# Second attention: GpSimd stores the outputs and makes the mLSTM's norm

## The chip, the cores and the metric

The kernel runs on one core of a Trainium2 chip. The metric is the device time of one execution in microseconds; for the kernel before it is 3558.35 us, the median of three runs (3557.78 to 3562.14).

## What is computed

Two transformer blocks on 2048 tokens of width 1024, all in float32. The first block (a Fourier branch beside grouped attention) and the end of the second (a mixture of experts and a gated embedding) are not touched. The part of the second block that matters here has two branches, whose outputs stand side by side and go through one output projection `w_o`:

```
def second_block(x, ...):
        attn_out = _mla_attention(q_nope, q_rope, k_nope, k_rope, v)   # 8 heads, mask in chunks of 64
        xc = jax.nn.silu(_causal_conv(x_m, conv_w[i], conv_b[i]))
        mq, mk, mv = (per head: xc @ w_mq, xc @ w_mk * 128**-0.5, x_m @ w_mv)      # 4 heads of 128
        hm = _mlstm_chunkwise(mq, mk, mv, ig, fg).transpose(0, 2, 1, 3)
        mu = jnp.mean(hm, axis=-1, keepdims=True)
        var = jnp.mean(jnp.square(hm - mu), axis=-1, keepdims=True)
        hm = ((hm - mu) * lax.rsqrt(var + EPS)).reshape(B, S, ML_W) * mh_norm_g[i]
        ml_out = (hm + ml_skip[i] * xc) * jax.nn.silu(z)
        x = x + jnp.concatenate([attn_out, ml_out], axis=-1) @ w_o[i]
```

## The kernel before

The program is a chain of phases; each is a Python generator, and the first steps of the next phase (its loads) are issued while the one before still runs. The change lies in `phase_g`, which computes both branches at once, and in `mlstm`, the generator that it steps beside itself.

**Attention.** A unit is one head and one block of 512 queries (32 units, `u`). A step is one tile of 128 keys of a unit (320 steps). In each step TensorE makes the scores in three matmuls (L1281 to L1283, into `ps`), ScalarE takes the exponential (L1285, `pe`) and rounds it (L1287, `ph`), VectorE makes the rest (L1294, `pl`), and four steps later TensorE multiplies with the values (L83 to L85, `acc`). Ahead of the scores TensorE and VectorE find the maximum of each query row (L1257 into `pmx`, L1258); its negative is sent by a small DMA from GpSimd's queue into a row of the query tile (L1272, `t<-nm`). When a unit is through, `ending` copies `acc` to `o` (L1316), turns the row of sums by DMA (L1319), takes reciprocals, sends them out and back as a broadcast (L1322, L1325, `rc`), multiplies on GpSimd (L1327) and stores to `MIX2` from SP's queue (L1329). The numbers that it yields say after how many steps each piece comes: nine in all.

**The mLSTM.** An item is one chunk of 128 tokens and two of the four heads (32 items, one about every nine steps). Its stages come at fixed steps after its first (`after`): `load` (four loads on SP's queue into a pool of three buffers), `decay` (L1533 on GpSimd), `project` (L1546; `qw` on GpSimd, L1552), `turn`, `weigh`, `combine` (L1587, L1588, which read `qw` and the state), `divide` (L1603), `update`, `center`, `square` (sums of squares on ScalarE, L1633), `spread` (variance on VectorE, L1639; power -0.5 on GpSimd, L1640), `shift` (L1646 on VectorE, `mv`), `norm` (L1653, two activations on ScalarE), `gate` (transposes on TensorE, L1661; skip term on GpSimd, L1665; L1666 on VectorE; product with the gate on GpSimd, L1667) and `store` (L1674, from SP's queue).

Every engine runs its own instructions in order, and so does each queue that issues DMAs. The order isn't quite that of the code: a scheduler in the framework places the instructions of each engine by its own estimates, with the code's order as the priority. When no step but the endings is left, `phase_g` closes its inner pools and starts the loads of `w_o` for the projection behind it (`e.beside(then)`).

Of the kernel before, what the change touches and what calls it, by code (L numbers as in the profile page):

```python
# [10 lines left out]
F32 = mybir.dt.float32  # L11
# [7 lines left out]
EPS = 1e-6  # L19
# [1109 lines left out]
def phase_g(e, then):  # L1129
# [20 lines left out]
    with ExitStack() as st:  # L1150
# [161 lines left out]
        def ending(u):  # L1312

            h, b = divmod(u, NB)
            o = wk.tile([65, QB], F32, name="o", bufs=3)
            nc.scalar.activation(o, A.pop(u), AF.Copy)  # L1316
            yield 1
            rr = sm.tile([16, QB // 16], F32, name="rr")
            nc.sync.dma_start(rr, o[64:65, :].rearrange("p (a b) -> p a b", a=16))  # L1319
            yield 2  # L1320
            nc.vector.reciprocal(rr, rr)
            nc.sync.dma_start(RD2[u].rearrange("(a b) -> a b", a=16), rr)  # L1322
            yield 2
            rc = wk.tile([64, QB], F32, name="rc", bufs=2)
            nc.sync.dma_start(rc, bcast_row(RD2[u], 64, QB))  # L1325
            yield 3
            nc.gpsimd.tensor_tensor(o[0:64], o[0:64], rc, op=ALU.mult)  # L1327
            yield 1
            nc.sync.dma_start(MIX2[h * 64:(h + 1) * 64, b * QB:(b + 1) * QB], o[0:64])  # L1329

# [9 lines left out]

        turns = []
        later = {}
# [25 lines left out]
        for n in range(-LEAD, len(steps) + LAG):  # L1368
# [15 lines left out]
            if beside and next(beside, True):  # L1384
                beside = None
            if not beside and not queue and not turns and not any(f is not step_ending for x in later.values() for f, a in x) and then:
                inner.close()
                e.beside(then)
                then = None
# [91 lines left out]
def mlstm(e, pool, psum, steps):  # L1481
# [12 lines left out]
    cst = pool("h_cst", 1)  # L1494
    xp = pool("h_x", 3)
    wk = pool("h_wk", 2)
# [5 lines left out]
    nc.gpsimd.memset(mask, 0.0)  # L1502
    nc.gpsimd.affine_select(out=mask, in_=mask, pattern=[[1, CL]], compare_op=ALU.is_ge, fill=-1e30, base=0, channel_multiplier=-1)
    taps = cst.tile([128, 4, 2], F32, name="taps")
    for i, n in enumerate(("mh_norm_g_2", "ml_skip_2")):
        nc.sync.dma_start(taps[:, :, i], d[n][0].rearrange("(h p) -> p h", p=128))
    state = [cst.tile([128, 130], F32, name=f"C{h}") for h in range(4)]
    for h in range(4):
        nc.gpsimd.memset(state[h], 0.0)
    wm = cst.tile([128, 3, 4, 128], F32, name="wm")  # L1510
    for i, n in enumerate(("w_mq_2", "w_mk_2", "w_mv_2")):
        nc.sync.dma_start(wm[:, i], d[n][0].rearrange("h d e -> d h e"))
    V.tensor_scalar(wm[:, 1], wm[:, 1], 128.0 ** -0.5, None, op0=ALU.mult)
    R = {}

    def load(x):
        ci, h0 = x
        t0 = ci * CL
        xm = xp.tile([128, 2, CL], F32, name="xm")
        xc = xp.tile([128, 2, CL], F32, name="xc")  # L1520
        for T, w in ((XM, xm), (XC, xc)):
            nc.sync.dma_start(w, T[h0 * 128:(h0 + 2) * 128].rearrange("(h p) s -> p h s", p=128)[:, :, t0:t0 + CL])
        negm = xp.tile([128, 2, CL], F32, name="negm")
        wint = xp.tile([128, 2, CL], F32, name="wint")
        for T, w in ((MR, negm), (WI, wint)):
# [110 lines left out]
    def spread(x):  # L1636

        xc, hm, mu, var, zs = R[x]
        V.tensor_scalar(var, var, 1.0 / CL, EPS, op0=ALU.mult, op1=ALU.add)  # L1639
        nc.gpsimd.tensor_tensor(var, var, e.mhalf[:, :2], op=ALU.pow)  # L1640
        R[x] = (xc, hm, mu, var, zs)

    def shift(x):
        xc, hm, mu, var, zs = R[x]
        mv = sm.tile([128, 2], F32, name="mv")
        V.tensor_mul(mv, mu, var)  # L1646
        R[x] = (xc, hm, mv, var, zs)

    def norm(x):
        ci, h0 = x  # L1650
        xc, hm, mv, var, zs = R[x]
        for i in range(2):
            nc.scalar.activation(hm[:, i], hm[:, i], AF.Identity, scale=var[:, i:i + 1], bias=mv[:, i:i + 1])  # L1653
        R[x] = (xc, hm, zs)

    def gate(x):
# [10 lines left out]
        nc.gpsimd.tensor_tensor(o, o, zs, op=ALU.mult)  # L1667
        R[x] = o

    def store(x):  # L1670
        ci, h0 = x
        o = R.pop(x)
        r = slice(512 + h0 * 128, 512 + (h0 + 2) * 128)
        nc.sync.dma_start(MIX2[r].rearrange("(h p) s -> p h s", p=128)[:, :, ci * CL:(ci + 1) * CL], o)  # L1674

    stages = (load, decay, project, turn, weigh, combine, divide, update, center, square, spread, shift, norm, gate, store)
    after = (0, 5, 7, 9, 11, 13, 14, 15, 15, 16, 17, 21, 22, 24, 26)
    items = [(ci, h0) for ci in range(NC) for h0 in (0, 2)]
# [811 lines left out]
```

## Time and profile before

| what | us |
|---|---|
| median of three runs | 3558.35 |
| the profiled execution, whole | 3560.11 |
| its span (first to last instruction) | 3558.4 |
| TensorE busy in the span | 3340.2 (94%) |
| VectorE, ScalarE, GpSimd busy | 2427.9, 2052.8, 688.9 |
| the stretch of `phase_g` | about 1918 to 2590 |

Busy time is a sum over the span; what limits the kernel in a stretch is read from what ended each engine's idle time there. An engine's wait is put down to the event that came last.

### The profile page before, as it was taken

Reading aid. Unit: us, or ns where it says so; the run is one execution under the profiler, and the core shown is the slowest. Engines: PE = TensorE matmul, PEld = TensorE weight load, DVE = VectorE, ACT = ScalarE, POOL = GpSimd, SP = SyncE. Lnnn points to the kernel's source line nnn. Section 1 sums busy time; section 2 is a strip of 40 time slices with the busy share of each in tenths; the row PEclk is TensorE's granted clock in tenths of the full one; section 3 lists DMA queues with packets and bytes.
Section 4 is the critical chain, followed back from the end, with each engine's and each line's share of the span. In section 5 each row is a group of like instructions: output and inputs, shape, how many; then the busy total and the mean of one; then the engine's idle time right before and its main releaser. Section 6 shows DMA issues by size and latency. Waiting matters only on the chain. (4 is left out here: it accounts for less than half of the span.)

```text
span 3558.4 us, 48779 instructions
## 1 busy us (share of the span) xinstructions
PE 3340.2 (94%) x16556; PEld 2592.6 (73%) x16557; DVE 2427.9 (68%) x4600; ACT 2052.8 (58%) x3672; POOL 688.9 (19%) x729
## 2 busy tenths in 40 slices
PE   8999999999999998999986998988999989899798
PEld 6788766666666666889975777766778767677687
DVE  5835768888888865464454887877856657877654
ACT  4442357777777783243223777877833467777533
POOL 0000000000000000000022433433200046655332
PEclk9999999999999998999997999999999989999999
DMA  5333322101111026443247533332255578878753
GB/s 160 102 122 105 95 71 72 51 22 54 34 45 44 26 63 197 146 139 112 75 127 187 106 79 77 84 69 60 83 167 167 211 263 309 342 301 302 276 195 130
DMA packets 312984, 468.82 MB, mean 132 GB/s; under 512 B 66455, under 2 KB 201384, under 8 KB 304416
## 3 DMA queue, kind: packets, MB, share of 16 engines
q1 hardware_dynamic: 293174, 404.26, 36.6%
q0 software_dynamic: 19520, 60.97, 4.7%
q8 instruction: 148, 2.42, 0.3%
q14 instruction: 142, 1.16, 0.1%
HBM read 333.81 MB, written 135.24 MB: 132 GB/s over the span
## 5 line engine op out<-in xcount | busy, mean ns | idle before, releaser
L519 DVE TENSOR_REDUCE mx<-pmx 128x1 f32<-128x512 f32 x512 | 344.5, 685 | 85.0 <-PE pmx L518 78.8
L588 DVE TENSOR_TENSOR pl<-pe,ph 128x1024 fp32r<-128x1024 f32 (+1 forms) x272 | 340.5, 1253 | 88.5 <-ACT ph L581 87.1
L579 ACT ACTIVATE pe<-ps 128x1024 f32<-128x1024 f32 (+1 forms) x272 | 278.7, 1025 | 147.2 <-PE ps L577 137.1
L581 ACT ACTIVATE ph<-pe 128x1024 fp32r<-128x1024 f32 (+1 forms) x272 | 287.4, 1058 | 7.4
L576 PE MATMUL ps<-t,kh 128*128 128x512 f32 (+1 forms) x544 | 239.6, 440 | 0.8 <-ACT pe L579 0.8
L1294 DVE TENSOR_TENSOR pl<-pe,ph 128x512 fp32r<-128x512 f32 (+1 forms) x320 | 211.6, 664 | 39.5 <-ACT ph L1287 36.9
L74 DVE TENSOR_TENSOR gl<-raw,gh 128x512 fp32r<-128x512 f32 x256 | 222.1, 915 | 19.0 <-ACT gh L73 18.6
L577 PE MATMUL ps<-t,kl 65*128 65x512 f32 (+1 forms) x544 | 222.9, 410 | 0.0
L602 PE MATMUL acc<-ph,vh 128*65 128x512 f32 (+1 forms) x544 | 217.5, 400 | 0.0
L604 PE MATMUL acc<-pl,vh 128*65 128x512 f32 (+1 forms) x544 | 215.1, 396 | 0.0
L603 PE MATMUL acc<-ph,vl 128*65 128x512 f32 (+1 forms) x544 | 215.0, 395 | 0.0
L518 PE MATMUL pmx<-kh,t 128*128 128x512 f32 x512 | 207.4, 410 | 1.7 <-DVE mx L519 1.1
L1258 DVE TENSOR_REDUCE mx<-pmx 128x1 f32<-128x512 f32 (+2 forms) x320 | 190.7, 598 | 9.1 <-PE pmx L1257 8.8
L1285 ACT ACTIVATE pe<-ps 128x512 f32<-128x512 f32 (+1 forms) x320 | 167.0, 523 | 30.7 <-PE ps L1283 27.5
L1287 ACT ACTIVATE ph<-pe 128x512 fp32r<-128x512 f32 (+1 forms) x320 | 179.5, 564 | 6.5
L74 POOL TENSOR_TENSOR dl<-sd,dh 128x512 fp32r<-128x512 f32 x128 | 165.4, 1313 | 80.4 <-ACT dh L73 77.8
L1281 PE MATMUL ps<-t,kh 113*128 113x512 f32 (+1 forms) x320 | 136.0, 425 | 35.7 <-ACT pe L1285 28.9
L83 PE MATMUL pm<-uhi,fh 128*128 128x256 f32 x512 | 146.0, 286 | 7.4 <-ACT ev L956 3.9
L73 ACT ACTIVATE gh<-raw 128x512 fp32r<-128x512 f32 x256 | 141.1, 621 | 13.0 <-PE p L85 9.4
L84 PE MATMUL pm<-ulo,fh 128*128 128x256 f32 x512 | 144.6, 283 | 0.0
L85 PE MATMUL pm<-uhi,fl 128*128 128x256 f32 x512 | 144.2, 284 | 0.3 <-DVE fl L77 0.3
L626 POOL TENSOR_TENSOR rc<-rc,ag 128x512 f32<-128x512 f32 x16 | 23.9, 1495 | 608.0 <-DMA rc<-scr_RD 561.6
(545 smaller groups left out, 9641.7 us busy)
## 6 DMA issues: line engine op xcount, KB each, us to landing
raw<-in_w_gate_e SPq DMA_DIRECT2D x32, 1024.0 KB
raw<-in_w_up_e SPq DMA_DIRECT2D x32, 1024.0 KB
sd<-in_w_down_e SPq DMA_DIRECT2D x32, 1024.0 KB
ws<-in_w_in SPq DMA_DIRECT2D x80, 256.0 KB
xt<-in_x SPq DMA_DIRECT2D x32, 512.0 KB
scr_X<-y SPq DMA_DIRECT2D x32, 512.0 KB
xt<-scr_X SPq DMA_DIRECT2D x32, 512.0 KB
yy<-scr_Y POOLq DMA_DIRECT2D x32, 512.0 KB, 4.7
```

Source lines behind the costliest of these rows:

```text
L74: (eng or nc.vector).tensor_tensor(lo, src, f32(hi), op=ALU.subtract)
L518: nc.tensor.matmul(p, t1[:, i * 128:(i + 1) * 128], kh[:, j * 512:(j + 1) * 512], start=True, stop=True)
L519: nc.vector.reduce_max(mx[:, i, j:j + 1], p, axis=AX.X)
L576: nc.tensor.matmul(p[:n, c], kh[:, k0:k0 + n], t1[:, c], start=True, stop=False)
L577: nc.tensor.matmul(p[:n, c], kl[:, k0:k0 + n], t2[:, c], start=False, stop=True)
L579: nc.scalar.activation(pe[:n], p[:n], AF.Exp, scale=0.125)
L581: nc.scalar.activation(ph[:n], pe[:n], AF.Copy)
L588: nc.vector.tensor_tensor(pl[:n], pe[:n], f32(ph[:n]), op=ALU.subtract)
L602: nc.tensor.matmul(A[u][j], vh[:n, i, :65], ph[:n, c], start=i == 0, stop=False)
L603: nc.tensor.matmul(A[u][j], vl[:n, i, :65], ph[:n, c], start=False, stop=False)
L604: nc.tensor.matmul(A[u][j], vh[:n, i, :65], pl[:n, c], start=False, stop=i == 16)
L1294: nc.vector.tensor_tensor(pl[:, c0:], pe[:, c0:], f32(ph[:, c0:]), op=ALU.subtract)
```

## The change

Four things are changed together.

1. `norm` moves from ScalarE to GpSimd, and `shift` falls away: `spread` now makes the scaled variance, the power and the two normalisations (add the negative mean, multiply by the root) as four GpSimd instructions in a row. `gate` comes at step 23 instead of 24.
2. The stores to `MIX2`, 32 of the attention and 32 of the mLSTM, are issued from GpSimd's queue right behind the product that makes their data, not from SP's some steps later.
3. The mLSTM's loads get four buffers instead of three. The three weight loads `wm` go to GpSimd's queue, the two small `taps` loads come behind the second item's loads, and the state is cleared by VectorE.
4. A unit's end is spread over fourteen steps instead of nine, with four `o` buffers; and the projection's start also waits until the last head's first unit has been stored (`NU - NB in done`).

```diff
         def ending(u):
...
-            o = wk.tile([65, QB], F32, name="o", bufs=3)
+            o = wk.tile([65, QB], F32, name="o", bufs=4)
             nc.scalar.activation(o, A.pop(u), AF.Copy)
-            yield 1
+            yield 2
             rr = sm.tile([16, QB // 16], F32, name="rr")
             nc.sync.dma_start(rr, o[64:65, :].rearrange("p (a b) -> p a b", a=16))
-            yield 2
+            yield 4
             nc.vector.reciprocal(rr, rr)
             nc.sync.dma_start(RD2[u].rearrange("(a b) -> a b", a=16), rr)
-            yield 2
+            yield 3
             rc = wk.tile([64, QB], F32, name="rc", bufs=2)
             nc.sync.dma_start(rc, bcast_row(RD2[u], 64, QB))
-            yield 3
+            yield 5
             nc.gpsimd.tensor_tensor(o[0:64], o[0:64], rc, op=ALU.mult)
-            yield 1
-            nc.sync.dma_start(MIX2[h * 64:(h + 1) * 64, b * QB:(b + 1) * QB], o[0:64])
+            nc.gpsimd.dma_start(MIX2[h * 64:(h + 1) * 64, b * QB:(b + 1) * QB], o[0:64])
+            done.append(u)
...
-            if not beside and not queue and not turns and not any(f is not step_ending for x in later.values() for f, a in x) and then:
+            if not beside and not queue and not turns and NU - NB in done and not any(f is not step_ending for x in later.values() for f, a in x) and then:
...
-    xp = pool("h_x", 3)
+    xp = pool("h_x", 4)
...
+        nc.gpsimd.dma_start(wm[:, i], d[n][0].rearrange("h d e -> d h e"))
...
-        nc.gpsimd.memset(state[h], 0.0)
-    wm = cst.tile([128, 3, 4, 128], F32, name="wm")
-    for i, n in enumerate(("w_mq_2", "w_mk_2", "w_mv_2")):
-        nc.sync.dma_start(wm[:, i], d[n][0].rearrange("h d e -> d h e"))
-    V.tensor_scalar(wm[:, 1], wm[:, 1], 128.0 ** -0.5, None, op0=ALU.mult)
+        V.memset(state[h], 0.0)
...
     def spread(x):
 
         xc, hm, mu, var, zs = R[x]
-        V.tensor_scalar(var, var, 1.0 / CL, EPS, op0=ALU.mult, op1=ALU.add)
-        nc.gpsimd.tensor_tensor(var, var, e.mhalf[:, :2], op=ALU.pow)
-        R[x] = (xc, hm, mu, var, zs)
-
-    def shift(x):
-        xc, hm, mu, var, zs = R[x]
-        mv = sm.tile([128, 2], F32, name="mv")
-        V.tensor_mul(mv, mu, var)
-        R[x] = (xc, hm, mv, var, zs)
-
-    def norm(x):
-        ci, h0 = x
-        xc, hm, mv, var, zs = R[x]
+        G = nc.gpsimd
+        G.tensor_scalar(var, var, 1.0 / CL, EPS, op0=ALU.mult, op1=ALU.add)
+        G.tensor_tensor(var, var, e.mhalf[:, :2], op=ALU.pow)
         for i in range(2):
-            nc.scalar.activation(hm[:, i], hm[:, i], AF.Identity, scale=var[:, i:i + 1], bias=mv[:, i:i + 1])
+            G.tensor_scalar(hm[:, i], hm[:, i], mu[:, i:i + 1], var[:, i:i + 1], op0=ALU.add, op1=ALU.mult)
         R[x] = (xc, hm, zs)
...
-    def store(x):
-        ci, h0 = x
-        o = R.pop(x)
         r = slice(512 + h0 * 128, 512 + (h0 + 2) * 128)
-        nc.sync.dma_start(MIX2[r].rearrange("(h p) s -> p h s", p=128)[:, :, ci * CL:(ci + 1) * CL], o)
...
+        nc.gpsimd.dma_start(MIX2[r].rearrange("(h p) s -> p h s", p=128)[:, :, ci * CL:(ci + 1) * CL], o)
...
-    after = (0, 5, 7, 9, 11, 13, 14, 15, 15, 16, 17, 21, 22, 24, 26)
+    after = (0, 5, 7, 9, 11, 13, 14, 15, 15, 16, 17, 23)
...
-            plan.setdefault(k * (steps - 28) // len(items) + a, []).append((f, x))
+            plan.setdefault(k * (steps - 25) // len(items) + a, []).append((f, x))
```

Three places show what the scheduler makes of it. In the names the digits tell tiles apart. First ScalarE in the middle of the phase, before, from an item's squares to its norm:

```order
L1633 ACTIVATE sq_20465,var_20466<-hm_20401,mu_20402 128x128
L1218 ACTIVATE t12_16806<-qf_20396 96x512
L1285 ACTIVATE pe_20452<-ps_20448 128x512
L1287 ACTIVATE ph_20454<-pe_20452 128x512
L1548 ACTIVATE qs_20474<-pmx_20469 128x256
L1550 ACTIVATE ks_20476<-pmx_20469 128x256
L1653 ACTIVATE hm_20401<-hm_20401,mv_20596,var_20466 128x128
L1285 ACTIVATE pe_20484<-ps_20480 128x512
L1653 ACTIVATE hm_20401<-hm_20401,mv_20596,var_20466 128x128
L1287 ACTIVATE ph_20486<-pe_20484 128x512
```

The norm stands five instructions behind the squares that it depends on. The same place with the change:

```order
L1634 ACTIVATE sq_20203,var_20204<-hm_20140,mu_20141 128x128 x2
L1549 ACTIVATE qs_20212<-pmx_20207 128x256
L1551 ACTIVATE ks_20214<-pmx_20207 128x256
L1285 ACTIVATE pe_20222<-ps_20218 128x512
L1287 ACTIVATE ph_20224<-pe_20222 128x512
L1285 ACTIVATE pe_20248<-ps_20244 128x512
L1287 ACTIVATE ph_20250<-pe_20248 128x512
```

Between the squares and the next scores nothing is left that comes from GpSimd. Second, GpSimd before, one item's worth:

```order
L1667 TENSOR_TENSOR o_20434<-o_20434,zs_20179 128x256
L1565 MEMSET v1_20768 128x2x2
L1640 TENSOR_TENSOR var_20466<-var_20466,mhalf_63 128x2
L1552 TENSOR_TENSOR qw_20478<-qs_20474,wint_20281 128x256
L1665 TENSOR_SCALAR o_21166<-xc_20526,taps_17346 128x128 x2
L1327 TENSOR_TENSOR o_20547<-o_20547,rc_20672 64x512
L1272 DMA t11_16805<-nm_20645 1x4x128
L1533 TENSOR_TENSOR negm_21556<-negm_21556,mask_17341 128x256
```

The power stands right behind the product of the gate and a small memset. With the change (two units end here, one shown):

```order
L1658 TENSOR_TENSOR o_19868<-o_19868,zs_19665 128x256
L1660 DMA scr_MIX2<-o_19868 128x2x128
L1534 TENSOR_TENSOR negm_21026<-negm_21026,mask_17341 128x256
L1656 TENSOR_SCALAR o_20641<-xc_20016,taps_17351 128x128 x2
L1641 TENSOR_SCALAR var_19926<-var_19926 128x2
L1642 TENSOR_TENSOR var_19926<-var_19926,mhalf_63 128x2
L1644 TENSOR_SCALAR hm_19875<-hm_19875,mu_19876,var_19926 128x128 x2
L1553 TENSOR_TENSOR qw_19962<-qs_19958,wint_19769 128x256
L1327 TENSOR_TENSOR o_19828<-o_19828,rc_20076 64x512
L1328 DMA scr_MIX2<-o_19828 64x512
```

`qw` now stands behind the whole norm, and the skip term (L1656) behind the store that frees its buffer: the three `o` buffers of the gate turn in a ring, and this one's turn is `o_19868`'s. Third, SP's queue before:

```order
L1325 DMA rc_20345<-scr_RD2 64x512
L1329 DMA scr_MIX2<-o_20195 64x512
L1526 DMA negm_21289<-scr_MR 128x2x128
L1674 DMA scr_MIX2<-o_20434 128x2x128
L1625 DMA zs_20928<-scr_ZS 128x2x128
L1210 DMA qf_21156<-scr_QNT 64x512
L1522 DMA xc_21033<-scr_XC 128x2x128
```

The loads of the coming items stand behind two stores that wait for GpSimd. With the change:

```order
L1325 DMA rc_20199<-scr_RD2 64x512
L1210 DMA qf_20696<-scr_QNT 64x512
L1211 DMA qf_20696<-scr_QRT 32x512
L1524 DMA negm_21281<-scr_MR 128x2x128
L1626 DMA zs_20913<-scr_ZS 128x2x128
L1319 DMA rr_20236<-o_20162 16x1x32
L1520 DMA xc_21023<-scr_XC 128x2x128
```

The stores are gone from it.

## Rows read from the trace of the kernel before

**Rows 1.** Busy us by stretch: PE, PEld, DVE, ACT, POOL; PE clock, DMA share, GB/s.

```profile
1918.00:2000.00 82.00, 61.84 (x306) 49.22 (x307) 55.78 (x133) 45.83 (x119) 28.11 (x39) 0.83 0.69 143
2000.00:2480.00 480.00, 438.29 (x2436) 341.34 (x2436) 386.24 (x908) 365.66 (x903) 170.32 (x221) 0.98 0.32 76
2480.00:2590.00 110.00, 106.04 (x546) 79.98 (x545) 94.00 (x198) 91.56 (x203) 23.65 (x32) 0.98 0.27 79
```

**Rows 2.** TensorE's waits, 2000 to 2500: line waited for, total us, times, longest.

```profile
PE ps L1281 <- ACT pe L1285: 25.5, 19, 3.5
PE pmx L1577 <- DVE mx L1258: 7.4, 2, 6.3
```

**Rows 3.** The longest waits of all engines, 2000 to 2500.

```profile
ACT hm L1653 <- DVE mv L1646: 70.1, 27, 8.3
POOL negm L1533 <- DMA negm<-scr_MR: 66.7, 14, 10.3
POOL o L1327 <- DMA rc<-scr_RD: 63.1, 15, 9.2
DVE mv L1646 <- POOL var L1640: 56.0, 25, 8.5
```

**Rows 4.** What SP's queue waited for, 2000 to 2500.

```profile
SPq L1674 <- POOL o L1667: 82.1, 20, 8.0
SPq L1329 <- POOL o L1327: 56.1, 23, 5.4
```

**Rows 5.** Timeline, one item: start, us, engine, instruction, idle before and its releaser.

```profile
2202.75 0.38 PE L1661 MATMUL pmx<-ident,hm 128*128 128x128 f32 x2
...
2205.19 0.73 POOL L1667 TENSOR_TENSOR o<-o,zs 128x256 f32<-128x256 f32 x1 [1.38 <-DVE o L1666]
...
2210.10 0.72 POOL L1640 TENSOR_TENSOR var<-var,mhalf 128x2 f32<-128x2 f32 x1
...
2210.85 0.33 DVE L1646 TENSOR_TENSOR mv<-mu,var 128x2 f32<-128x2 f32 x1 [2.97 <-POOL var L1640]
...
2211.22 0.49 ACT L1653 ACTIVATE hm<-hm,mv,var 128x128 f32<-128x128 f32 x1 [1.98 <-DVE mv L1646]
...
2214.37 0.50 PE L1281 MATMUL ps<-t,kh 113*128 113x512 f32 x1 [1.01 <-ACT pe L1285]
```

**Rows 6.** Groups by line: count, busy us, mean ns of one, idle before it.

```profile
L1653 ACT ACTIVATE hm<-hm,mv,var 128x128 f32<-128x128 f32 x64 | 30.6, 487 | 73.4 <-DVE mv L1646 73.4
```

**Rows 7.** The same for GpSimd, from its list.

```profile
L1665 POOL TENSOR_SCALAR o<-xc,taps 128x128 f32<-128x128 f32 x64 | 50.9, 802 | 35.9 <-DMA scr_MIX<-o 17.5 <-DMA xc<-scr_XC 14.0 <-issue 2.5
L1327 POOL TENSOR_TENSOR o<-o,rc 64x512 f32<-64x512 f32 x32 | 45.3, 1414 | 119.7 <-DMA rc<-scr_RD 99.1 <-ACT pe L1285 16.9 <-PE ps L1283 3.7
L92 POOL TENSOR_TENSOR ss<-ss,mhalf 128x1 f32<-128x1 f32 (+1 forms) x48 | 30.4, 636 | 442.8 <-DVE ss L91 318.2 <-DVE ss L106 120.0 <-ACT junk L868 4.6
L1667 POOL TENSOR_TENSOR o<-o,zs 128x256 f32<-128x256 f32 x32 | 28.6, 893 | 35.0 <-DVE o L1666 19.6 <-DVE mu L1623 15.4
L1552 POOL TENSOR_TENSOR qw<-qs,wint 128x256 f32<-128x256 f32 x32 | 25.4, 794 | 5.2 <-ACT qs L1548 3.5 <-DMA wint<-scr_WI 1.6
L1640 POOL TENSOR_TENSOR var<-var,mhalf 128x2 f32<-128x2 f32 x32 | 24.9, 778 | 5.7 <-DVE var L1639 4.6 <-ACT ks L1550 0.8
L1272 POOL DMA_DIRECT2D t<-nm x32 | 19.6, 613 | 89.9 <-DVE nm L1271 49.0 <-DVE vl L1201 20.8 <-DVE pl L1294 10.9
```

**Rows 8.** GpSimd's own DMA issue of `t<-nm`: ns min/median/max, then us to landing.

```profile
L1272 POOL DMA_DIRECT2D t<-nm x32: 518/627/633, 1919.0 to 2559.0; - x32
...
DMA to landing us min/median/max: 1.6/2.8/8.8
```

**Rows 9.** A larger DMA from GpSimd's queue, later in the kernel: KB each, us to landing.

```profile
yy<-scr_Y POOLq DMA_DIRECT2D x32, 512.0 KB, 4.7
```

**Rows 10.** Timeline at the start of the phase.

```profile
1918.97 0.62 POOL L1272 DMA_DIRECT2D t<-nm  x1 [2.45 <-DVE nm L1271]
...
1924.49 0.80 PE L1281 MATMUL ps<-t,kh 113*128 113x512 f32 x1 [5.78 <-DMA t<-nm]
```

More of the change, by code (lines that the diff above doesn't have):

```diff
@@ L1339, in phase_g @@
         beside = mlstm(e, top, lambda: pmx.tile([128, 512], F32, name="pmx"), len(steps) + LEAD - REST)
-        turns = []
+        turns, done = [], []
         later = {}
@@ L1503, in mlstm @@
     nc.gpsimd.affine_select(out=mask, in_=mask, pattern=[[1, CL]], compare_op=ALU.is_ge, fill=-1e30, base=0, channel_multiplier=-1)
+    wm = cst.tile([128, 3, 4, 128], F32, name="wm")
+    for i, n in enumerate(("w_mq_2", "w_mk_2", "w_mv_2")):
+        nc.gpsimd.dma_start(wm[:, i], d[n][0].rearrange("h d e -> d h e"))
+    V.tensor_scalar(wm[:, 1], wm[:, 1], 128.0 ** -0.5, None, op0=ALU.mult)
     taps = cst.tile([128, 4, 2], F32, name="taps")
-    for i, n in enumerate(("mh_norm_g_2", "ml_skip_2")):
-        nc.sync.dma_start(taps[:, :, i], d[n][0].rearrange("(h p) -> p h", p=128))
     state = [cst.tile([128, 130], F32, name=f"C{h}") for h in range(4)]
     for h in range(4):
-        nc.gpsimd.memset(state[h], 0.0)
-    wm = cst.tile([128, 3, 4, 128], F32, name="wm")
-    for i, n in enumerate(("w_mq_2", "w_mk_2", "w_mv_2")):
-        nc.sync.dma_start(wm[:, i], d[n][0].rearrange("h d e -> d h e"))
-    V.tensor_scalar(wm[:, 1], wm[:, 1], 128.0 ** -0.5, None, op0=ALU.mult)
+        V.memset(state[h], 0.0)
     R = {}
@@ L1526, in load @@
             nc.sync.dma_start(w, bass.AP(tensor=T.tensor, offset=T.offset + (h0 * NC + ci) * CL, ap=[[0, 128], [NC * CL, 2], [1, CL]]))
+        if x == items[1]:
+            for i, n in enumerate(("mh_norm_g_2", "ml_skip_2")):
+                nc.sync.dma_start(taps[:, :, i], d[n][0].rearrange("(h p) -> p h", p=128))
         R[x] = (xc, xm, negm, wint)
@@ L1667, in gate @@
         nc.gpsimd.tensor_tensor(o, o, zs, op=ALU.mult)
-        R[x] = o
-    def store(x):
-        ci, h0 = x
-        o = R.pop(x)
         r = slice(512 + h0 * 128, 512 + (h0 + 2) * 128)
-        nc.sync.dma_start(MIX2[r].rearrange("(h p) s -> p h s", p=128)[:, :, ci * CL:(ci + 1) * CL], o)
-    stages = (load, decay, project, turn, weigh, combine, divide, update, center, square, spread, shift, norm, gate, store)
-    after = (0, 5, 7, 9, 11, 13, 14, 15, 15, 16, 17, 21, 22, 24, 26)
+        nc.gpsimd.dma_start(MIX2[r].rearrange("(h p) s -> p h s", p=128)[:, :, ci * CL:(ci + 1) * CL], o)
+    stages = (load, decay, project, turn, weigh, combine, divide, update, center, square, spread, gate)
+    after = (0, 5, 7, 9, 11, 13, 14, 15, 15, 16, 17, 23)
     items = [(ci, h0) for ci in range(NC) for h0 in (0, 2)]
```

## The prediction

> **What bounds the kernel now.** I read the stretch table first, since the change touches one phase only. In `phase_g` TensorE is the busiest engine: from 2000 to 2480 us it is busy 438.3 of 480 us at a mean granted clock of 0.98, ScalarE 365.7, VectorE 386.2, GpSimd 170.3; before 2000 it runs at 0.83 and is busy 61.8 of 82 us [rows 1]. So the most that any edit of the waiting can give back in the middle is TensorE's 41.7 idle us and a clock loss of 0.02 x 480 = 9.6 us.
>
> Then TensorE's own waits, for what ended them: 25.5 us in 19 waits for the exponential (L1285, on ScalarE), and 7.4 us in 2 for a maximum (L1258, on VectorE) [rows 2], together 32.9 of the 41.7 us. Neither engine is short of time by its busy share, so the next view is what they wait for themselves. ScalarE waits 70.1 us in 27 pieces for `mv` in front of the norm; VectorE waits 56.0 us in 25 in front of `mv` for GpSimd's power [rows 3]. One item shows how these hang together: the power runs on GpSimd at 2210.10, VectorE had idled 2.97 us for it before it made `mv` at 2210.85, ScalarE had idled 1.98 us when the norm began at 2211.22, and at 2214.37 TensorE had been without an exponential for 1.01 us [rows 5]. **A four-step chain of two-element work stops three in-order engines once per item**, with the exponentials and maxima of the attention queued behind it.
>
> Why GpSimd is late for the power, with 170 of 480 us busy: it waits 66.7 us for the load of `negm` and 63.1 for `rc` [rows 3], with everything behind these in its queue. And those loads are late since SP's queue waits 82.1 and 56.1 us for GpSimd's products in front of the two stores [rows 4]. GpSimd waits for a load that SP issues only after a store that waits for GpSimd.
>
> **The change part by part.** *The norm off ScalarE and VectorE.* ScalarE loses 64 activations of 487 ns, 30.6 us [rows 6], and its 70.1 us of waiting; VectorE the 56.0 us. Neither is on the end's path by itself; what counts is TensorE's 32.9 us. All of it is the upper bound. What is late next is VectorE, busy 386.2 of 480 us [rows 1], or TensorE itself; if half a microsecond of the usual small waits stays in each of the 27 items, 13.5 us remain and 19.4 are won. I take 26, the middle, since both of the engines that TensorE waited for are freed at once.
>
> *The clock.* Up to 9.6 us in the middle, nothing at the least. The low clock stands beside the stretches with idling [rows 1]; with most of the stops gone I take 6.
>
> *The norm on GpSimd.* Nearest rows: a 128x128 multiplication by a column, 802 ns (the new form has two columns), a tiny instruction 636 ns, the power 778 as now [rows 7]. That is 2 x 0.80 + 0.64 = 2.24 us more per item. *The stores on GpSimd.* Its DMA issue costs 613 ns in the mean [rows 7]; 64 of them make 39 us, beside 32 x 2.24 = 72 us for the norm. Together 111 us on an engine that was busy 222 of the 672 us of the phase (28.11 + 170.32 + 23.65 [rows 1]). By load alone that fits; the question is the order.
>
> *GpSimd's chain per item.* The scheduler puts the skip term of a later item behind the store that frees its buffer, the norm behind that, and `qw`, which TensorE needs for the item after next's combination, behind the norm. From the transposes of an item to its product on GpSimd 2205.19 - 2202.75 = 2.44 us [rows 5]; product 0.89, issue 0.61 [rows 7]; landing 2.8 us, the median of the small DMA that goes the same way [rows 8] (the mask's addition and a memset lie inside it); skip term 2 x 0.80, scale 0.64, power 0.78, norm 2 x 0.80, `qw` 0.79 [rows 7]. Sum 12.2 us; with the end of a unit between (product 1.41, two issues of 0.61 [rows 7]) 14.8. In the code that is from step 23 of one item to step 13 of the next but one, 2 x 9.28 - 10 = 8.56 steps. The phase runs 672 us over 342 steps, 1.96 us each, so TensorE gives it 16.8 us now and 16.0 when it is faster by as much as I forecast. It fits by a margin of 1.2 us in the worse items. Of the landing alone no row shows this size: 1.6 us at the least and 8.8 at the most for 2 KB [rows 8], and 4.7 for 512 KB in a quieter part [rows 9]; 2.8 is of this phase, hence taken. For items in which the margin is used up I add **+6 us** (0.2 for each of 30); from 0 to the rivals below.
>
> The Trainium skill speaks against this part. [...] "SBUF — State Buffer", section "SBUF: two separate sides", says that a DMA from GpSimd's queue stalls while VectorE holds the port pair that both share, since GpSimd can't write its descriptors then. What this would make of the time is the first rival's 3578.
>
> *SP's queue without stores; four load buffers.* The 138 us that SP waits for GpSimd go, and loads are issued earlier. What that saves GpSimd, it saves in front of the chain above; on TensorE it is in the 26 us already. *Fourteen steps for a unit's end.* The pauses only give the three DMAs more room; with a fourth `o` buffer nothing waits for them, except at the end of the phase: the projection's first tile needs the last head's first unit, and that comes five steps later, 9.8 us if uncovered. It is covered, I think, by the 16 weight loads of `w_o` and the steps still to run: in ScalarE's order the conversion of that tile stands 31 instructions behind the unit's copy before, and 30 with the change. 0, with +9.8 as the bound.
>
> *The start.* TensorE waits 5.78 us there for the first `t<-nm`, issued on GpSimd at 1918.97 [rows 10]. Now three weight loads go ahead of it in that queue (3 x 0.61 us of issue, and their data), while SP comes to the first item's loads five issues sooner. Between -5.8 (the wait goes) and +5.8 (it doubles); 0.
>
> **Sum:** -26 - 6 + 6 = -26 us on the profiled execution's 3560.1, which is 1.8 us above the median of the three runs: 3560.1 - 1.8 - 26 = **3532 us**. At best -32.9 - 9.6 - 5.8 = -48, 3510.
>
> **Rivals.** *GpSimd's chain becomes the bound (slower).* If the stores land late, the skip term waits for its buffer, and norm and `qw` wait behind it; TensorE then waits for `qw` or for the transposes' input. The point is a landing of 2.8 + (16.8 - 14.8) = 4.8 us: from there the items with a unit's end are slower than today's. At 5.5 us they lose 0.7 us each, some 20 us over 30 items, with nothing gained: 3578. For it: one such DMA took 8.8 us to land [rows 8], and the margin is small. Against: 32 issues in this very phase took 518 to 633 ns, none stretched [rows 8]. 11%. By the Trainium skill's rule on the shared port (above) it would be the likely case; the even issue speaks against that.
>
> *The gain is eaten (same).* The landing is about that of the larger DMA, 4.7 us [rows 9]: the chain takes 14.1 and 16.7 us, as long as TensorE gives it today, so the items keep today's pace, and the wait is on TensorE's combination instead of on ScalarE's norm. Some 3 us remain from items without a unit's end: 3555. For it: the store is 128 KB in 256 rows, nearer to that DMA in kind than 2 KB. 17%.
>
> *The edits don't take hold:* the scheduler could have left the norm where ScalarE still waits, or put the loads as late as before. The orders show neither; I give it no chance of its own.
>
> **How the numbers follow.** The forecast's own range, 3518 to 3549, gets 60%; more (both engines freed fully and the clock back, 3506 to 3518) 12%; the eaten gain 17%, the slower case 11%. Faster by over 0.2% (7 us, about what a measurement of this kernel can tell from no change) is 0.60 + 0.12 = 0.72, within it 0.17, slower 0.11. The range 3510 to 3562 leaves out the slower case and a part of the best one, and takes in the bounds of the start and of the end; since cases that gain hold most of the chance, its lower half is the likelier.
>
> **What would show it.** Right: in the changed profile ScalarE has no wait for `mv` and none for GpSimd beyond a few us; VectorE's 56.0 us are gone; TensorE's waits for L1285 fall under 10 us from 2000 on; SP shows no wait for a GpSimd product; the mean clock is 0.99 or 1.00; and `phase_g` ends some 26 us earlier while the phases behind it keep their length. Wrong: waits of TensorE for the norm's output or for `qw`, GpSimd's skip term (L1656) waiting over 2 us per item for a store, or issues over 1 us in GpSimd's queue would mean that its chain has taken over; waits of TensorE on VectorE in their place would mean that the 26 us were set too high. A longer gap before the first scores would put the start's 0 at fault, and one before the projection's first tile the end's.

## The result and the profile after

The change made the kernel slower by 0.5%: 3577.06 us (median of 6 runs, 3573.89 to 3584.24) against 3560.24 of the kernel before on the same chip, a ratio of 1.0052 with a 95% interval of 1.0034 to 1.007. Forecast were 3532 us. The profiled execution took 3578.93 us (span 3577.2, mean granted clock 0.967; before 3558.4 and 0.975).

Where the 18.8 us of span lie: `phase_g` starts at the same time and its last accumulation ends 14.4 us later; the rest, some 4 us, is lost at the projection's start and in the phases behind. First the stretch table (columns as in [rows 1]), the phase before and then after, and the middle after:

```profile
1918.00:2590.00 672.00, 606.17 (x3284) 470.54 (x3285) 536.02 (x1238) 503.04 (x1223) 222.09 (x290) 0.96 0.36 85
```

```profile
1918.00:2604.40 686.40, 614.45 (x3284) 481.72 (x3285) 526.20 (x1173) 488.82 (x1158) 332.59 (x450) 0.92 0.31 82
2000.00:2480.00 480.00, 433.93 (x2338) 342.05 (x2337) 366.15 (x825) 342.01 (x814) 250.94 (x336) 0.93 0.29 75
```

The same 3284 matmuls are busy 8.3 us longer (614.45 - 606.17), since the clock is lower (0.92 against 0.96), and TensorE is idle 6.1 us longer (71.9 against 65.8). Together that is the 14.4 us. The wait for the first scores alone grew by 8.3 us (5.78 to 14.03, below); without it TensorE idles 57.9 us, 2.1 less than before (60.0). So past the start the loss is one of the clock, not of idle time. Next the waits from 2000 to 2500, TensorE's first, then the longest of VectorE, SP and GpSimd, to be laid beside [rows 2 to 4]:

```profile
PE ps L1281 <- DMA t<-nm: 17.0, 4, 5.9
PE pmx L1269 <- DVE m L1263: 11.0, 3, 4.3
PE pmx L1614 <- DVE mx L1258: 6.0, 2, 3.6
PE pmx L1257 <- DVE mx L1258: 5.6, 3, 4.2
PE pmx L1589 <- POOL qw L1553: 3.1, 2, 2.1
...
DVE rr L1321 <- DMA rr<-o: 47.9, 14, 7.1
...
SPq L1524 <- POOL qw L1553: 130.4, 24, 9.1
SPq L1626 <- POOL o L1658: 73.4, 22, 6.9
...
POOL o L1327 <- DMA rc<-scr_RD: 71.9, 17, 10.1
POOL negm L1534 <- DMA negm<-scr_MR: 35.8, 9, 12.0
POOL o L1658 <- DVE o L1657: 32.6, 11, 7.1
POOL o L1656 <- DMA scr_MIX<-o: 32.2, 16, 5.1
```

What was to go has gone: no wait of TensorE for an exponential is among them (25.5 us in [rows 2]), VectorE's 56.0 us for `mv` and ScalarE's 70.1 [rows 3] don't exist, SP has no store to wait for. In their place stand others. **VectorE waits 47.9 us at `rr`**, the reciprocals of a unit's sums, which cost it 8.2 us before; **SP waits 130 us for `qw`** in front of loads; and TensorE has 12 waits for `nm`, `m` and `mx`, 3.3 us each in the mean, where it had 19 of 1.3 us for exponentials. The row of before for `rr`, 2000 to 2500:

```profile
DVE rr L1321 <- DMA rr<-o: 8.2, 6, 2.3
```

The end of one unit shows both new chains (start, us, engine, instruction, idle before it and its releaser). ScalarE wrote the unit's sums at 2157.25; SP issues the transfer `rr` at 2163.17, behind the load `zs` that waits for a gate's product. VectorE, in order, stands 3.90 us, `m` behind it is late, and so is the transpose that waits for `m`. Then SP issues `rc` at 2171.66, behind the load `wint`, which waits for a `qw` of GpSimd's. GpSimd stands 5.23 us for `rc`, with the store and two `nm` behind it in its queue. The first of these was written at 2168.64 and is issued at 2179.59, and the first scores of a later unit wait for it:

```profile
2157.25 0.59 ACT L1316 ACTIVATE o<-acc 65x512 f32<-65x512 f32 x1
...
2162.70 0.38 SPq L1626 DMA_DIRECT2D zs<-scr_ZS  x1
2163.17 0.54 SPq L1319 DMA_DIRECT2D rr<-o  x1
...
2165.50 0.34 DVE L1321 RECIPROCAL rr<-rr 16x32 f32<-16x32 f32 x1 [3.90 <-DMA rr<-o]
...
2166.42 0.17 DVE L1263 TENSOR_REDUCE m<-mx 128x4 f32<-128x16 f32 x1
...
2166.64 0.27 PE L1269 MATMUL pmx<-ident,m 128*4 128x128 f32 x1 [2.69 <-DVE m L1263]
...
2168.64 0.27 DVE L1271 TENSOR_SCALAR nm<-pmx 4x128 fp32r<-4x128 f32 x1
...
2169.81 1.37 POOL L1553 TENSOR_TENSOR qw<-qs,wint 128x256 f32<-128x256 f32 x1
...
2171.20 0.36 SPq L1524 DMA_DIRECT2D wint<-scr_WI  x1
2171.66 0.46 SPq L1325 DMA_DIRECT2D rc<-scr_RD  x1
...
2176.84 1.84 POOL L1327 TENSOR_TENSOR o<-o,rc 64x512 f32<-64x512 f32 x1 [5.23 <-DMA rc<-scr_RD]
...
2178.98 0.61 POOL L1328 DMA_DIRECT2D scr_MIX<-o  x1 [0.29 <-POOL o L1327]
2179.59 1.09 POOL L1272 DMA_DIRECT2D t<-nm  x2
...
2181.63 0.77 PE L1281 MATMUL ps<-t,kh 113*128 113x512 f32 x1 [5.89 <-DMA t<-nm]
...
2182.20 0.63 PE L1282 MATMUL ps<-t,kh 96*128 96x512 f32 x1
```

The last row is the third thing to see: this matmul of 512 columns takes 0.63 us, where the granted clock is 0.50 (1.2 GHz, from 2177.8 to 2188.1); with the clock at 1.00 (2.4 GHz) it takes 0.40. From 1915 to 2620 the profile has 11 such stretches before, 54.6 us together, and 16 after, 107.7 us. Beside each of the 16 stands one wait of TensorE of 2.1 to 14.0 us; the one from 2427.0 begins 1.4 us ahead of its wait, behind two of 0.2 and 0.9 us for the norm's output. From 2000 to 2500 TensorE has 11 waits of over 2 us, where it had 4. It is no strict rule: before, two of the stretches (from 2215.4 and 2570.4) have only waits of up to 1.5 us ahead of them, and a wait of 2.2 us (until 2232.9) has no stretch beside it.

The start (to be compared with [rows 10]): VectorE's scale of the key weights stands ahead of the first `nm` and waits for weights that now come by GpSimd's queue; the first scores start 8.3 us later than before.

```profile
1925.37 0.43 DVE L1507 TENSOR_SCALAR wm<-wm 128x512 f32<-128x512 f32 x1 [7.21 <-DMA wm<-in_w_mk]
...
1925.71 0.27 DVE L1271 TENSOR_SCALAR nm<-pmx 4x128 fp32r<-4x128 f32 x1
...
1926.28 0.56 POOL L1272 DMA_DIRECT2D t<-nm  x1 [8.10 <-DVE nm L1271]
...
1932.76 0.80 PE L1281 MATMUL ps<-t,kh 113*128 113x512 f32 x1 [14.03 <-DMA t<-nm]
```

### The profile page after: what moved, and what is told of

Read it like the earlier page. It is cut to its first block, busy times and chain, and to the rows that moved or that the text cites. A ratio compares the mean times of both kernels' runs of the same rounds, so it can differ in the third digit from the quotient of the medians.

```text
span 3577.2 us, 48915 instructions
## 1 busy us (share of the span) xinstructions
PE 3351.0 (94%) x16556; PEld 2605.0 (73%) x16557; DVE 2420.1 (68%) x4540; ACT 2040.1 (57%) x3608; POOL 799.7 (22%) x888
## 5 line engine op out<-in xcount | busy, mean ns | idle before, releaser
L588 DVE TENSOR_TENSOR pl<-pe,ph 128x1024 fp32r<-128x1024 f32 (+1 forms) x272 | 342.5, 1260 | 86.7 <-ACT ph L581 85.3
L538 POOL DMA_DIRECT2D t<-nm x16 | 9.0, 563 | 683.4 <-DMA scr_AG<-ev 446.9
L73 ACT ACTIVATE gh<-raw 128x512 fp32r<-128x512 f32 x256 | 141.1, 621 | 14.9 <-PE p L85 9.4
```

What stands on the lines that cost most here:

```text
L588: nc.vector.tensor_tensor(pl[:n], pe[:n], f32(ph[:n]), op=ALU.subtract)
```

## The experiments

Each ratio is to runs of the kernel before made beside it on the same chip; from set to set the median of that kernel went from 3560 to 3572 us, so ratios are compared, not times. By the intervals, a difference of two ratios is uncertain by 0.002 to 0.0025, some 7 to 9 us. The other columns are of the one profiled run: VectorE's wait at `rr` (us, 2000 to 2480), TensorE's waits for `nm` past the start (1960 to 2600; us, count), stretches with a granted clock of 0.50 from 1915 to 2620 (count, us). One run need not be a typical one: a_rract's is the slowest of its 12 (3591.77 us, the median is 3573.01), a_stsp's the fastest of its 5. SyncE in the expectations is SP.

| kernel | ratio, 95% | at `rr` | for `nm` | lower clock |
|---|---|---|---|---|
| before | 1 | 8.2 | 1.0, 1 | 11, 54.6 |
| after | 1.0052 (1.0034 to 1.0070) | 47.9 | 17.0, 4 | 16, 107.7 |
| a_start | 1.0024 (1.0012 to 1.0037) | 58.4 | 14.6, 4 | 18, 102.4 |
| a_nmact | 1.0027 (1.0009 to 1.0045) | 57.4 | none | 12, 91.9 |
| a_xp3 | 1.0047 (1.0030 to 1.0063) | 56.4 | 13.9, 4 | 15, 92.2 |
| a_end9 | 1.0041 (1.0025 to 1.0057) | 58.8 | 12.6, 3 | 12, 78.5 |
| a_stsp | 1.0055 (1.0040 to 1.0071) | 59.4 | 12.5, 4 | 15, 99.0 |
| a_rract | 1.0017 (1.0001 to 1.0032) | 9.2 | 16.3, 5 | 13, 85.3 |
| a_best1 | 0.9968 (0.9955 to 0.9981) | 5.0 | none | 14, 71.7 |
| a_stsp_rr_start | 0.9994 (0.9981 to 1.0006) | 11.6 | 18.8, 4 | 15, 78.5 |
| b_norm | 1.0002 (0.9987 to 1.0018) | 60.7 | 2.3, 2 | 15, 80.4 |
| b_st | 1.0048 (1.0031 to 1.0066) | 7.4 | none | 17, 88.7 |
| b_norm_rract | 0.9943 (0.9927 to 0.9959) | 14.6 | 11.5, 2 | 9, 64.9 |
| b_norm_rr_st | 0.9928 (0.9911 to 0.9945) | 19.8 | 3.3, 2 | 7, 44.4 |
| b_norm_rr_nm | 0.9918 (0.9901 to 0.9934) | 18.8 | none | 11, 64.9 |
| b_norm_rr_e14 | 0.9955 (0.9940 to 0.9970) | 16.6 | 13.9, 3 | 11, 64.9 |
| b_norm_rr_x4 | 0.9952 (0.9937 to 0.9966) | 10.9 | 12.1, 3 | 8, 54.6 |
| b_norm_rr_e14x4 | 0.9953 (0.9938 to 0.9968) | 18.1 | 15.1, 5 | 11, 58.0 |
| b_norm_rr_plan | 0.9975 (0.9961 to 0.9989) | 14.9 | 13.4, 3 | 12, 68.3 |
| b_best | 0.9922 (0.9908 to 0.9936) | 16.4 | none | 8, 41.0 |

**The start, and the queue of `nm`.** In a_start the mLSTM's weights, taps and states are set up as before (the hunk with `wm`, `taps` and `state` undone). In a_nmact only this line differs from the changed kernel:

```diff
-            nc.gpsimd.dma_start(t1[DH:MR_, :].rearrange("p (a b) -> p a b", b=128), nm)
+            nc.scalar.dma_start(f32(t1[DH:MR_, :]).rearrange("p (a b) -> p a b", b=128), f32(nm))
```

> The changed kernel with the second attention's start as before: the mLSTM's weights and taps loaded on SyncE's queue, the states cleared on GpSimd. Theory START (the scale of the weights stands ahead of nm on VectorE and waits for weights that now come over GpSimd's queue until 1925.37, so the first scores wait 14.0 us instead of 5.8): the wait goes back to about 6 us, 8 us less, 3569 us, and the rest of the stage keeps its loss. Theory QUEUE (nm's transfer stands in GpSimd's queue behind instructions that wait or take long, at the units with four blocks of keys): the waits of the first scores for nm further on (17.0 us in 4, plus 18.2 in 5 that the view puts down to issue, in 2000 to 2480) stay, so 3565 to 3572. If START were all of it, 3560.

> The changed kernel with nm's transfer issued on ScalarE's queue instead of GpSimd's, nothing else. Theory QUEUE: nm is issued when VectorE has written it, the waits of the first scores past the start fall from 35 us to under 8, the granted clock of 2000 to 2480 rises from 0.93 to 0.97 or more, and the time falls by 12 to 25 us to 3552 to 3565, although ScalarE gets 32 issues. The start keeps its 14 us there, as nm is late on VectorE itself. Rival CLOCK (the clock is lower for another reason than these waits): under 5 us less, 3572 to 3580, with the clock still at 0.93.

a_start: first scores after a wait of 5.85 us, and the ratio 0.0028 lower, some 10 us, beside the 8 expected; the other loss stays. a_nmact: as expected no wait for `nm` is left past 1960, but the clock of 2000 to 2480 came only to 0.95 and the time fell by 9 us, short of the 12 expected: TensorE's waits on VectorE (`m`, `mx`) grew in their place, from 23 to 35 us. GpSimd's queue is a cause, not the whole. The 35 us for `nm` in the two expectations count the same stops twice: TensorE's matmuls wait 17.0 us in 4, and the 18.2 us put down to issue are the waits of the weight loads at the same 4 places and one more.

**The norm alone, and where `rr` is issued.** b_norm is the kernel before with `spread` of the change (and so without `shift` and `norm`); b_norm_rract and a_rract move one transfer in that kernel and in the changed one:

```diff
-            nc.sync.dma_start(rr, o[64:65, :].rearrange("p (a b) -> p a b", a=16))
+            nc.scalar.dma_start(rr, o[64:65, :].rearrange("p (a b) -> p a b", a=16))
```

> The kernel before with the norm on GpSimd alone (variance, power and two passes over hm there); stores, buffers, start and the unit's end as before. The step of the prediction: ScalarE no longer waits 70 us for mv, TensorE's 32 us of waits for the exponentials fall under 8, 3535 to 3548. Rival NORM (GpSimd's 1.7 to 2.5 us more an item puts nm late by itself): TensorE waits for nm over 15 us past the start, the clock of 2000 to 2480 falls under 0.96, 3558 to 3575.

> The kernel before with the norm on GpSimd, and rr issued on ScalarE's queue; the rest as before. With the norm alone the time was level (1.0002) and VectorE stood 61 us at the reciprocals in place of 55 us for mv. Theory VECTOR: those 61 us fall under 15, TensorE's waits for m, mx, den and qw from about 45 us to under 25, and the gain that the prediction put on the norm (20 us) comes out in part: 0.994 to 0.998. Rival: GpSimd's longer item itself is the limit (waits for qw and nm stay): 0.999 to 1.002.

> The changed kernel with one transfer moved: rr (the unit's row of sums, which VectorE takes the reciprocals of) is issued on ScalarE's queue behind the copy that writes it, not on SyncE's. Theory VECTOR (SyncE issues rr late, behind loads that wait for their buffers; VectorE, in order, stands 48 us at the reciprocals; m, mx and den behind them are late, TensorE has single waits of 2 to 6 us for these, and runs at the lower clock after each): VectorE's wait at rr falls under 12 us, TensorE's waits for m and mx from 24 us to under 10, its stretches at the lower clock from 15 to 10 or fewer, and the time falls by 8 to 18 us against the changed kernel, to a ratio of 0.9995 to 1.003 of the kernel before; the start keeps its 14 us. Rival QUEUE (GpSimd's queue holds nm): the waits for nm past the start stay over 15 us and the time falls under 5 us.

The norm alone gave nothing (1.0002): the forecast's step missed, and the rival met the time but not the cause, as TensorE waits 2.3 us for `nm`. TensorE's and VectorE's waits in b_norm, 2000 to 2500:

```profile
PE pmx L1269 <- DVE m L1263: 13.6, 3, 8.1
PE pmx L1588 <- POOL qw L1552: 10.1, 3, 3.7
PE pmx L1651 <- DVE den L1592: 7.1, 1, 7.1
...
DVE rr L1321 <- DMA rr<-o: 61.4, 17, 10.0
```

The waits for exponentials are away, but VectorE stands 61 us at `rr` and passes it on. With `rr` on ScalarE's queue, the same view:

```profile
PE ps L1281 <- DMA t<-nm: 11.5, 2, 6.7
PE pmx L1588 <- POOL qw L1552: 11.2, 7, 3.4
PE ps L1281 <- ACT pe L1285: 1.8, 2, 1.6
...
DVE rr L1321 <- DMA rr<-o: 14.6, 9, 3.2
```

That one line is worth 0.0059, 21 us; with it the norm's move brings 20 us against the kernel before, of the 26 that were forecast for it. From 2000 to 2500 TensorE's waits of over 2 us are 9 in b_norm and 4 in b_norm_rract. What no run separates is `rr`'s move from the norm's: there is none with `rr` on ScalarE's queue and the norm as before. That it would gain little there is argued from before's row for `rr`, 8.2 us. In the changed kernel the same line gives 0.0035, 12 us, and TensorE's waits for `m` and `mx` fall to 2.1 us (under 10 were expected); waits for `qw` come in their place (29.7 us in 11 from 1960 to 2600), `nm`'s stay, and 13 stretches at the lower clock are left, where 10 or fewer were expected. So VECTOR holds for the norm, and a second cause is in the changed kernel alone.

**The stores.** b_st has the two stores on GpSimd's queue and nothing else of the change; b_norm_rr_st adds them to b_norm_rract; a_stsp puts them back on SP's queue in the changed kernel, at the place in the code where the change has them.

> The kernel before with the two stores on GpSimd's queue and nothing else (ScalarE still makes the norm, three buffers, the unit's end over nine steps). By the prediction, stores alone take SyncE's 137 us of waits for them away, so the loads of negm come earlier (GpSimd's 67 us for negm under 45), and cost GpSimd about 0.6 us each: 0.997 to 1.000. Rival QUEUE: nm stands behind the stores that GpSimd issues, and TensorE waits for nm over 15 us past the start: 1.002 to 1.005.

> The kernel before with the norm on GpSimd and rr issued on ScalarE's queue (which measured 0.9943), and now the two stores on GpSimd's queue as well. Theory STORES (a store in GpSimd's queue takes GpSimd 0.6 to 0.8 us, and the next item's product into the slot waits there for the store's landing, so qw, behind it, is late and TensorE waits for qw): TensorE's waits for qw rise from 11 us to 25 or more, GpSimd's waits for its slot from none to about 40 us, and the ratio is 0.997 to 1.002. Rival: stores are neutral once rr is off SyncE's queue, and SyncE gains from being without them (201 us of waits for the two products there): 0.992 to 0.996.

> The changed kernel with the stores alone put back on SyncE's queue. Theory STORES: GpSimd's waits for its slot (31 us in 15) go, nm and qw are less late, but VectorE's 48 us at rr stay or grow, as SyncE has the stores again; 5 to 12 us under the changed kernel, ratio 1.001 to 1.004. Rival: what the stores give SyncE back is worth more than what they cost GpSimd: 1.005 to 1.009.

The same move costs 17 us on the kernel before and nothing that the intervals can tell on the other two (0.9943 to 0.9928; 1.0055 to 1.0052). In b_st the norm is still ScalarE's, and GpSimd's order is store, skip term, `qw`, power; the skip term waits there for its buffer until a store has landed, and everything that hangs on the power waits along (timeline of b_st):

```profile
2140.85 0.81 POOL L1674 DMA_DIRECT2D scr_MIX<-o  x1 [0.30 <-POOL o L1667]
...
2145.18 1.19 POOL L1665 TENSOR_SCALAR o<-xc,taps 128x128 f32<-128x128 f32 x2 [3.52 <-DMA scr_MIX<-o]
...
2147.03 0.72 POOL L1640 TENSOR_TENSOR var<-var,mhalf 128x2 f32<-128x2 f32 x1
...
2147.79 0.16 DVE L1646 TENSOR_TENSOR mv<-mu,var 128x2 f32<-128x2 f32 x1 [4.57 <-POOL var L1640]
...
2147.99 0.49 ACT L1653 ACTIVATE hm<-hm,mv,var 128x128 f32<-128x128 f32 x1 [5.00 <-DVE mv L1646]
...
2149.56 0.48 PE L1281 MATMUL ps<-t,kh 113*128 113x128 f32 x1 [4.19 <-ACT pe L1285]
```

With the norm on GpSimd, VectorE and ScalarE stand in that chain no more, and the stores cost nothing; that the one is the reason of the other is argued, not shown. It isn't `rr`'s move, since a_stsp and the changed kernel both have `rr` on SP's queue. My theory STORES fell with b_norm_rr_st (TensorE waits 12.0 us for `qw`, GpSimd 15.3 us for its slot from 2000 to 2500) and a_stsp (within the interval of the changed kernel); QUEUE's number for b_st came out, but not by its mechanism: there is no wait for `nm`. Nor did the loads of `negm` come earlier in b_st, as the prediction has it: GpSimd waits 88.9 us for them, beside 66.7 [rows 3].

**The four buffers, the fourteen steps and the plan.** a_xp3 and a_end9 take buffers and steps out of the changed kernel; the others add parts to b_norm_rract, or (a_stsp_rr_start) undo the stores and the start and move `rr`. b_norm_rr_plan has only this:

```diff
-    after = (0, 5, 7, 9, 11, 13, 14, 15, 15, 16, 17, 24, 26)
+    after = (0, 5, 7, 9, 11, 13, 14, 15, 15, 16, 17, 23, 23)
...
-            plan.setdefault(k * (steps - 28) // len(items) + a, []).append((f, x))
+            plan.setdefault(k * (steps - 25) // len(items) + a, []).append((f, x))
```

> The changed kernel with three buffers for the mLSTM's inputs as before. Theory BUFFERS (with four, loads are issued further ahead and stand in SyncE's queue for the buffer they wait for, 130 us in 24 for negm and wint; the reciprocals' transfers rr and rc come behind them, GpSimd waits 72 us for rc, and nm behind that): GpSimd's wait for rc falls under 50 us, VectorE's wait for rr from 48 to under 15, the waits of the first scores for nm fall by half or more, 3560 to 3568. If the queue of GpSimd fills from its own longer work (norm and stores) and not from SyncE's, the time stays within 5 us of 3577 and nm stays late.

> The changed kernel with the stores on SyncE's queue and the start as before, and rr issued on ScalarE's queue: of the change, the norm, the four buffers and the unit's end over fourteen steps are left. Theory STORES: it comes near the kernel before with norm and rr alone, 0.992 to 0.997, and TensorE's waits for qw are under 15 us. Rival BUFFERS and fourteen steps (loads issued ahead and waiting in SyncE's queue cost by themselves): 0.998 to 1.002.

> The kernel before with the norm on GpSimd and rr issued on ScalarE's queue (0.9943), and of the rest of the change only the unit's end over fourteen steps, with its fourth buffer for o. Theory STEPS (with the end spread, the product o by rc stands in GpSimd's queue ahead of nm at the units with four blocks of keys, and waits there for rc): TensorE's waits for nm past the start are 12 us or more in 3 or more, the ratio 0.997 to 1.001. Rival BUFFERS: no change, 0.992 to 0.996, and waits for nm as without it (11.5 us in 2).

> The kernel before with the norm on GpSimd and rr issued on ScalarE's queue (0.9943), and of the rest of the change only the four buffers for the mLSTM's inputs. Theory BUFFERS (loads are issued ahead and stand in SyncE's queue for their buffer, with rr's store and rc behind them): SyncE's wait for qw rises from 44 us to 100 or more, 0.997 to 1.001. Theory STEPS: 0.992 to 0.996, and SyncE's waits within 30 us of what they were.

> The changed kernel with the unit's end over nine steps and three buffers for o, as before, everything else as changed (rr on SyncE's queue, nm on GpSimd's). Theory STEPS: nm is no longer behind the product that waits for rc, TensorE's waits for nm past the start fall from 35 us to under 12, 1.000 to 1.003; VectorE's wait at rr stays over 40 us and the start keeps its 14 us. Rival BUFFERS: 1.004 to 1.007.

> The kernel before with the norm on GpSimd and rr issued on ScalarE's queue (0.9943), and of the rest of the change only the mLSTM's plan: an item's gate and store at step 23 instead of 24 and 26, and the items spread over three steps more. Theory PLAN (the new plan puts loads and the gate's products where SyncE and GpSimd wait for qw): SyncE's waits for qw rise from 44 us to 80 or more, TensorE's waits for qw and nm from 23 us to 35 or more, 0.997 to 1.000. Rival TOGETHER (it takes four buffers and fourteen steps at once): 0.992 to 0.996.

> The kernel before with the norm on GpSimd and rr issued on ScalarE's queue, with the four buffers and the unit's end over fourteen steps at once, and the mLSTM's plan as before. Theory TOGETHER: 0.998 to 1.000, SyncE's waits for qw 100 us or more and TensorE's for nm 15 us or more. Theory PLAN: 0.994 to 0.997, with these waits under 60 and under 15 us.

Three theories in a row fell here. Buffers: SP's wait for `qw` did not come down in a_xp3 (139 us) nor go up in b_norm_rr_x4 (43). Steps: neither a_end9 nor b_norm_rr_e14 moved by more than the interval. Together: 0.9953. The three additions to b_norm_rract all lie 0.0009 to 0.0012 above it, 3 to 4 us, which the intervals can't tell from nothing. What is left between b_norm_rr_e14x4 (0.9953) and a_stsp_rr_start (0.9994) is the plan alone, and it costs 0.0041 there and 0.0032 on b_norm_rract: 11 to 15 us. PLAN's ratio and SP's wait came as expected; TensorE's waits for `qw` and `nm` rose to 28.6 us only, where 35 were. Beside it in the trace of b_norm_rr_plan, SP's, TensorE's and GpSimd's waits, 2000 to 2500:

```profile
SPq L1526 <- POOL qw L1552: 114.6, 21, 11.1
...
PE pmx L1588 <- POOL qw L1552: 15.2, 6, 3.3
PE ps L1281 <- DMA t<-nm: 13.4, 3, 5.6
PE pmx L1257 <- DVE mx L1258: 5.1, 1, 5.1
...
POOL o L1657 <- DVE o L1656: 34.3, 11, 5.4
```

The gate comes a step earlier, and GpSimd stands 34.3 us in 11 for VectorE's half of it (11.5 in 5 without), with `qw` and `nm` in the same queue. That this is how the plan costs time is read from the trace, not shown: gate, store and the items' spacing were moved at once, and b_norm_rr_st has 70 us of SP's waits for `qw` without harm.

**Joined.** a_best1 is the changed kernel with its start undone and `rr` and `nm` on ScalarE's queue; b_norm_rr_nm and b_best join what gained.

> The changed kernel with the start as before, rr and nm issued on ScalarE's queue. If the three losses are what was read (start 8 us, nm in GpSimd's queue, VectorE at rr), they come off together: first scores wait 6 us, no wait of TensorE for nm past the start over 2 us, VectorE's wait at rr under 12 us, the clock of 2000 to 2480 at 0.97 or more: 25 us under the changed kernel, a ratio of 0.995 to 0.999 of the kernel before. Rival CLOCK or ScalarE as the new limit (64 issues of about 0.6 us): 1.000 to 1.004.

> The kernel before with the norm on GpSimd, rr and nm issued on ScalarE's queue. Theory QUEUE: the two waits of the first scores for nm that were left with rr alone (6.7 and 4.8 us, each with a stretch of 5.0 and 6.6 us at the lower clock behind it) go, about 15 us of the profiled run's stage: 0.990 to 0.993. Rival: ScalarE's 32 more issues of about 0.6 us come back as waits for exponentials: 0.994 to 0.997.

> The kernel before with the norm and the two stores on GpSimd, and rr and nm issued on ScalarE's queue; start, buffers and the unit's end as before. The two additions to norm and rr measured 0.9928 (stores) and 0.9918 (nm) one at a time against 0.9943. If they add up: 0.989 to 0.992, about 3533 to 3543 us. Rival: they take the same waits away, 0.992 to 0.994.

a_best1 lies 0.0084 under the changed kernel, 30 us, and beats the kernel before; its clock from 2000 to 2480 came to 0.96 only. b_norm_rr_nm and b_best are the fastest, 28 to 29 us under the kernel before (0.9918 and 0.9922, not told apart: the additions do not add up, as b_best's rival has it). a_best1 and b_best differ in the four buffers, the fourteen steps and the plan, 0.0046 or 16 us, which fits the plan's price. The stretch 2000 to 2480 of b_best, where TensorE gets through 2596 matmuls, 2436 before and 2338 with the change:

```profile
2000.00:2480.00 480.00, 457.48 (x2596) 363.58 (x2595) 408.31 (x910) 374.90 (x899) 262.06 (x343) 0.99 0.30 78
```

## Why the prediction was wrong, step by step

- **What bounds it, and the norm (-26).** This is the main step that failed. The chain through `mv` was read rightly and it went, but the norm alone gave nothing (b_norm, 1.0002): VectorE stood 61 us at `rr` instead. With `rr` moved as well 20 us came, within 19.4 to 32.9. What the prediction had wrong is "what is late next": I named VectorE by its busy share, and the sum has no term for what VectorE waits for when `mv` is gone. From 2000 to 2480 before, SP issued `rr` 0.92 us in the mean after the end of ScalarE's copy, and VectorE came to the reciprocals 4.74 us after it. In b_norm SP issued it after 2.35 us and VectorE came after 4.08; with the change after 2.72 and 4.38. So VectorE came a little sooner, and the transfer itself was issued later, the larger part. Why SP comes to it later in b_norm is not shown. The row of before (`rr`, 8.2 us in 6) isn't in the prediction.
- **The clock (-6, "nothing at the least").** The bound had the wrong sign: the matmuls took 8.3 us more. I took less idling to mean a higher clock; past the start TensorE does idle 2.1 us less, at a lower clock. What goes with the clock in these rows is the longer single wait: over 2 us there are 4 before and 11 after. This is read from the traces; no run changes the length of the waits alone.
- **GpSimd's chain (+6).** The prices were right but for one store's issue. Norm per item 2 x 0.78 + 0.44 + 0.90 = 2.9 us beside 3.0; store issues 0.80 (the mLSTM's) and 0.60 beside 0.61; landing 2.7 us in the median beside 2.8. TensorE's waits for `qw` and the norm are 4 us. What failed is that I listed only `qw` and the transposes as TensorE's customers of that queue. `nm` is the third, and cost 17.0 us in 4.
- **SP's queue.** "The 138 us go, and loads are issued earlier" was half of it: the loads then waited in the same queue, with `rr` and `rc` behind them.
- **Gate at step 23 and items spread wider.** No term of the sum; measured +11 to +15 us on two bases, both with `rr` on ScalarE's queue.
- **Fourteen steps, four buffers, the end (0).** Right: each moved the time by no more than its interval. At the projection's first tile TensorE waits 4.3 us instead of 2.2.
- **The start (0, bound 5.8).** +8.3 us, outside the bound. I counted GpSimd's issues, not who waits for the data: VectorE's scale, ahead of `nm`.
- **The rivals.** The slower one gave 3578, close to the result, by luck: its mechanism did not occur. It wanted stores that land late and TensorE waiting for `qw`; 9 of the 64 stores took over its 4.8 us, but the skip term's waits for a store are 37.3 us in 19, 1.2 us an item, and TensorE's for `qw` and the norm the 4 us above. The rule of the Trainium skill beside it ("SBUF — State Buffer", section "SBUF: two separate sides": a DMA of GpSimd's stalls while VectorE runs one of its two-port modes) is not seen either: `nm`'s issues took 537 to 642 ns, beside 518 to 633 before. No run shows in which mode VectorE's instructions ran, so that this was the likely case by the rule, as the prediction has it, was not established.

The sum that the runs give: norm 0 as long as `rr` is on SP's queue, plan +11 to +15, start +8 to +10, stores, buffers and steps about 0: 19 to 25 us beside the 17 measured, each difference uncertain by 7 to 9. It takes the plan to cost as much with `rr` on SP's queue; no run has the changed kernel with the plan of before. On the changed kernel itself the old start, `rr` and `nm` give 10, 12 and 9 us one at a time, and all three (a_best1) 30.

## What to carry to other kernels

When a wait is taken off an in-order engine, go through the other instructions on that engine that hang on transfers: the one whose input comes next latest can inherit the wait, and small rows of such waits are the ones to price. For every queue that gets more work, list all that the busiest engine takes from it, not only the tiles of the edit. And judge a part on the kernel in which it will stand: the stores cost 17 us without the norm's move and nothing with it.

## What the runs showed of the hardware

Runs of one and the same kernel differed by as much as the change itself, along with the clock: a_nmact took 3562.66 us at a mean granted clock of 0.976 and 3586.94 at 0.968. And the time at the lower level does not go by idle time as a whole: in the phase TensorE's idle time rose by 6.1 us from 65.8, the time with a granted clock of 0.50 from 51.2 to 105.8 us (a part of it while TensorE stood in the start's wait).
